# The gate of the second sub-layer applied to the last product instead of to w2 beside the scans

## The chip, the cores and the metric

The kernel runs on one core of a Trainium2 chip, as one program. The metric is the device time of one execution in microseconds (us). Three executions of the kernel before gave 2477.98, 2481.02 and 2481.66 us, so the median is 2481.02 us.

## The reference, cut to what matters

One layer of a hybrid backbone: two token mixers side by side (a bidirectional SSD branch and a bidirectional RG-LRU branch), merged and projected, then a squared-ReLU MLP. Each sub-layer is modulated at its input and gated at its output. All arrays are float32; there are 1024 latent tokens, 1024 model columns and 4096 hidden columns.

```python
def sq_relu_mlp(h, p):
    return jnp.square(jax.nn.relu(h @ p['w_mlp1'] + p['b_mlp1'])) @ p['w_mlp2'] + p['b_mlp2']

mx = [m[:, None, :] for m in modulation(c, w_mod[l], b_mod[l], N_MOD)]
x_mix, _ = token_mixer(modulate(x, mx[0], mx[1]), p, ctx_states, rows, True)
x = layer_norm(DEEPNORM_ALPHA * x + mx[2] * x_mix, ln1_g[l], ln1_b[l])
x = layer_norm(DEEPNORM_ALPHA * x + mx[5] * sq_relu_mlp(modulate(x, mx[3], mx[4]), p), ln2_g[l], ln2_b[l])
```

The change is about `mx[5]`, a row of 1024 numbers, one per model column. It may multiply the columns of `w_mlp2` (called w2 below) ahead of the product, or the columns of the product behind it.

## The kernel before, in words

A matrix product in float32 is made of three TensorE matmuls on split operands (`mm3`, L112): each operand is split into a high part (ScalarE, a copy to fp32r) and a low part (VectorE, a subtraction), and high x high, high x low and low x high are summed in PSUM. TensorE is written PE, VectorE DVE, ScalarE ACT, GpSimd POOL and SyncE SP in the profile's rows. All DMAs of the kernel are issued by SP, in one order.

The work runs in stages, one behind the other, and a scheduler mixes neighbouring stages by priorities. Each engine then executes its own list strictly in the order that the scheduler wrote.

1. The modulation vectors, the first layer norm and the first tiles of the input projection (to about 90 us).
2. The RG-LRU branch (to about 446 us). `mod_chunk` (L386) leaves `mx[5]` in the DRAM row `drow[1]`.
3. The SSD scans (L489 to L595, about 446 to 1363 us): eight groups `g`. A group projects and convolves B, C, two X tiles and z (`proj`, `conv_silu`), and then treats its two X tiles in turn (`tl` 0 and 1). `to_token` (L445) transposes a tile on PE, four 128x128 blocks at a time, into `misc`, the only PSUM buffer of that tag; a DVE copy (L452) moves each batch into `xtm`, and PE can't write the next batch before that. Then come the chunk states `H`, and for each half the decay tiles: SP loads `R` (L549, two buffers, 512 KB), POOL masks it (L554), ACT makes `L` from it (L559), DVE makes `M` (L562, L563), PE multiplies.
4. `gate_w2` (L481) is called at the end of each half of each tile, 32 times: it loads two halves of a 128x1024 tile of w2, multiplies each by the gate row `mxg` on DVE (L486) and stores it to the DRAM tile `dw2[m]`. The halves go through the pool `evp`, which has four 128x512 buffers under the tag `ev`, shared with every other short-lived tile.
5. The SSD product, the LRU product, the merge, the output projection, the second layer norm and the first MLP product (1363 to 2142 us). Its result goes to the DRAM tiles `da`.
6. The second MLP product (2142 to 2475 us) over 32 k tiles. `FRONT` (k tiles 0 to 3) goes first, each of the 16 result tiles as one plain sum over four k tiles (`direct`, L1080); its result is added on DVE to ALPHA times the residual `dx1` (L1097). `PAIRS` (k tiles 4 to 23) goes through `wino`, a seven-product scheme. `TAIL[0]` (24 to 27) and `TAIL[1]` (28 to 31) are plain sums again, added on DVE at L1130 and L1134, and after L1134 comes the last layer norm of that row of tiles. `TAIL[0]` uses the four PSUM buffers `acc`, `TAIL[1]` the three buffers `y`.

`whole` (L1055) and `halves` (L1065) load and split operands for the plain sums, as 128x1024 tiles or as halves. `hook` (L1117) starts the loads of the tails.

Of the kernel before, what the change touches and what calls it, by code (L numbers as in the profile page):

```python
# [9 lines left out]
F32 = mybir.dt.float32  # L10
F32R = mybir.dt.float32r
AF = mybir.ActivationFunctionType
OP = mybir.AluOpType
# [8 lines left out]
ALPHA = 2.0 ** 0.25  # L22
# [33 lines left out]
def _ap(t, off, dims):  # L56
    return bass.AP(tensor=t.tensor, offset=t.offset + off, ap=dims)
# [3 lines left out]
def tile_hybrid_layer(ctx: ExitStack, tc: tile.TileContext, x, xc, wmod, win, wdt, lruw, wbs, wbl,  # L61
# [411 lines left out]
        proj(win[T_Z + t], (0, 1), zcb)  # L473


    dw2 = [dr.tile([128, 1024], F32, name=f"dw{m}") for m in range(32)]
    mxg = [evp.tile([128, 512], F32, tag="ev", name="mxg") for _ in range(2)]
    for h_ in range(2):
        Q.dma_start(mxg[h_], _ap(drow, 1024 + h_ * 512, [[0, 128], [1, 512]]))

    def gate_w2(m):  # L481
        for h_ in range(2):
            sl = slice(h_ * 512, h_ * 512 + 512)
            t_ = evp.tile([128, 512], F32, tag="ev", name="wg")
            Q.dma_start(t_, w2[m][:, sl])
            V.tensor_tensor(t_, t_, mxg[h_], op=OP.mult)  # L486
            Q.dma_start(dw2[m][:, sl], t_)

    z_tile(0)  # L489
    for g in range(8):  # L490
        bf = gp.tile([128, TT], F32, name="bf", bufs=1)
        proj(win[T_B + g], (0, 1, 2), conv_silu(16 + g, bf))
        bt = gp.tile([128, 10, 128], F32, name="bt", bufs=1)
# [15 lines left out]
        for tl in range(2):  # L509
# [29 lines left out]
            for hf_ in range(2):  # L539
# [41 lines left out]
                if tl == 1:  # L581
                    V.tensor_tensor(sq, sq, sqs[0, hf_], op=OP.add)
                    pend.append((g, hf_, sq))
                gate_w2(4 * g + 2 * tl + hf_)
        if g < 7:
            z_tile(2 * g + 2)
            flush()
# [433 lines left out]

    rw0 = ctx.enter_context(tc.tile_pool(name="rw0", bufs=10, reuse_waits="tile"))
    opr = ctx.enter_context(tc.tile_pool(name="opr", bufs=NOP, reuse_waits="tile"))
    ac = ctx.enter_context(tc.tile_pool(name="mlc", bufs=16, side="right", reuse_waits="tile"))
# [9 lines left out]
    def raw1():  # L1036
        return rg.tile([128, 1024], F32, tag="k1", name="k1", bufs=10)
# [11 lines left out]
        return t_  # L1049

    def load_w2(m, t_):
        Q.dma_start(t_, dw2[m])
        return t_

    def whole(m, get):  # L1055

        o_ = []
        for ld in (load_a, load_w2):
            lo, hi = ld(m, get()), get().bitcast(F32R)
            A.activation(hi, lo, AF.Copy)  # L1060
            V.tensor_tensor(lo.bitcast(F32R), lo, hi.bitcast(F32), op=OP.subtract)
            o_.append([(hi[:, h_ * 512:h_ * 512 + 512], lo.bitcast(F32R)[:, h_ * 512:h_ * 512 + 512]) for h_ in range(2)])
        return o_

    def halves(m, pool, tags, bufs):  # L1065
        o_ = []
        for src, (th_, tl_) in zip((da, dw2), tags):
            w_ = []
            for h_ in range(2):
                hi = pool.tile([128, 512], F32R, tag=th_, name=th_, bufs=bufs)  # L1070
                lo = pool.tile([128, 512], F32R, tag=tl_, name=tl_, bufs=bufs)
                raw = lo.bitcast(F32)
                Q.dma_start(raw, src[m][:, h_ * 512:h_ * 512 + 512])
                A.activation(hi, raw, AF.Copy)
                V.tensor_tensor(lo, raw, hi.bitcast(F32), op=OP.subtract)
                w_.append((hi, lo))
            o_.append(w_)
        return o_

    def direct(ops, i, n_, tag="acc", bufs=4):  # L1080
        pt = ps.tile([128, 512], F32, tag=tag, bufs=bufs, name="mo")
        ts_ = slice(i % 4 * 128, i % 4 * 128 + 128)
        for j, (la, rb) in enumerate(ops):
            mm3(pt, la[i // 4][0][:, ts_], la[i // 4][1][:, ts_], rb[n_][0], rb[n_][1], j == 0, j == len(ops) - 1)
        return pt

    with tc.high_priority(offset=60):
        front = [halves(m, mhA, (("mhh", "mhl"), ("mhh", "mhl")), 8) for m in FRONT[:2]]
        front += [whole(m, raw1) for m in FRONT[2:]]
    pre = {}  # L1090
    for r_, c_ in ((0, 0), (1, 0), (0, 1), (1, 1)):
        pre[r_, c_] = [ac.tile([128, 512], F32, name="ma", bufs=16) for i in range(4)]
        for i in range(4):
            t_ = pre[r_, c_][i]
            Q.dma_start(t_, dx1[r_ * 4 + i][:, c_ * 512:c_ * 512 + 512])
            pt = direct(front, r_ * 4 + i, c_)
            V.scalar_tensor_tensor(t_, t_, ALPHA, pt, op0=OP.mult, op1=OP.add)  # L1097

    accs = [pre[{2: (0, 0), 4: (1, 0), 3: (0, 1)}[n]] if n in (2, 4, 3) else
            [mhA.tile([128, 512], F32, tag="mhh" if n in (1, 5) else "mhl", name="ma", bufs=8) for i in range(4)]  # L1100
# [7 lines left out]
        V.tensor_tensor(pre[1, 1][i], pre[1, 1][i], t_, op=OP.add)  # L1108
        return pre[1, 1][i]

    tail = [[], []]

    def tail_raw():
        n0[0] += 1
# [2 lines left out]
    def hook(n):  # L1117
        if n == 7:
            for t_, n_ in ((ln2g, "ln2g"), (ln2b, "ln2b")):
                Q.dma_start(t_, _ap(rows, ROWS[n_] * 1024, [[0, 128], [1, 1024]]))  # L1120
            tail[0] = [whole(m, tail_raw) for m in TAIL[0]]
        else:
            tail[1] = [whole(m, raw1) for m in TAIL[1][:2]]
            tail[1] += [halves(m, opr, (("olh", "oll"), ("orh", "orl")), NOP) for m in TAIL[1][2:]]

    wino(PAIRS, chunks, raw0, raw1_or_w, opr, load_a, load_w2, accs, (2, 3, 4), fin, hook, add5, on=V, bank=1)
    for r_, c_ in ((1, 1), (0, 0), (1, 0), (0, 1)):
        for i in range(r_ * 4, r_ * 4 + 4):
            pt = direct(tail[0], i, c_)
            V.tensor_tensor(macc[i][c_], macc[i][c_], pt, op=OP.add)  # L1130
    for i in (0, 4, 1, 5, 2, 6, 3, 7):
        for n_ in range(2):
            pt = direct(tail[1], i, n_, "y", 3)
# [53 lines left out]
```

## Time and profile before

| what | us |
|---|---|
| median of three runs | 2481.02 |
| the profiled execution | 2482.07 |
| its span | 2480.0 |
| PE busy | 2365.0 |
| DVE busy | 1907.8 |
| ACT busy | 1101.3 |
| POOL busy | 415.7 |

The span is the stretch between the first and the last instruction of the profiled execution; 2.07 us lie around it. A busy engine can still be at less than its full pace: a matmul's row is longer than the time until the next one starts, so a busy time of PE is an upper bound. PEclk is the share of the 2.4 GHz clock that TensorE was granted in a stretch, 1.00 for all of it and 0.5 for a stretch at 1.2 GHz.

### The profile page before, as it was taken

To read this page: it belongs to the slowest core of one execution; us is meant where nothing else is said; L and a number is where in the kernel's file an instruction comes from. 1 tells how busy PE (TensorE), PEld (TensorE's weight loads), DVE (VectorE), ACT (ScalarE), POOL (GpSimd) and SP (SyncE) were. 2 spreads that over 40 slices of the span, in tenths; PEclk is the share of its full clock that TensorE was granted. 3 is DMA by queue.
4 is the path that set the end of the run, shared out by engine and by line. 5 is a ranking of instruction groups with operands and counts; after the bars stand their busy time and mean duration, and the time that the engine had idled before them with its cause. 6 is when DMAs were issued, how large, how long until landed. Compare 5 with 4: busy or idle time off the path is not lost. (4 is left out here: it accounts for less than half of the span.)

```text
span 2480.0 us, 31785 instructions
## 1 busy us (share of the span) xinstructions
PE 2365.0 (95%) x11437; PEld 1888.3 (76%) x11437; DVE 1907.8 (77%) x3206; ACT 1101.3 (44%) x1927; POOL 415.7 (17%) x357
## 2 busy tenths in 40 slices
PE   7999999999999999999999998899979999999998
PEld 3877788777777777777877877677757888788877
DVE  6976788778888888879788489977787555558976
ACT  3666756434343443434344254332245545435521
POOL 1000000001110110101110156600365322000004
PEclk9999999999999999999999999999989999999999
DMA  7322154544544453534333632267224332823121
GB/s 283 127 58 73 56 162 145 174 151 126 176 125 136 130 154 117 167 95 119 93 91 118 230 109 90 77 209 266 85 78 156 119 111 98 295 104 144 43 68 68
DMA packets 149382, 324.11 MB, mean 131 GB/s; under 512 B 16468, under 2 KB 49364, under 8 KB 149224
## 3 DMA queue, kind: packets, MB, share of 16 engines
q1 hardware_dynamic: 149224, 322.08, 40.5%
q8 instruction: 90, 1.47, 0.2%
q14 instruction: 68, 0.56, 0.1%
HBM read 256.41 MB, written 65.61 MB: 130 GB/s over the span
## 5 line engine op out<-in xcount | busy, mean ns | idle before, releaser
L114 PE MATMUL acc<-hl,wh 128*128 128x512 f32 (+1 forms) x1560 | 600.2, 385 | 0.6 <-DVE hl L182 0.6
L113 PE MATMUL acc<-hh,wh 128*128 128x512 f32 (+1 forms) x1560 | 598.2, 384 | 2.4 <-ACT hh L177 2.4
L115 PE MATMUL acc<-hh,wl 128*128 128x512 f32 (+1 forms) x1560 | 597.9, 383 | 0.0
L113 PEld LDWEIGHTS acc<-hh,wh 128*128 128x128 f32 x1560 | 298.4, 191 | 54.2 <-issue 4.1
L114 PEld LDWEIGHTS acc<-hl,wh 128*128 128x128 f32 x1560 | 298.3, 191 | 53.4 <-issue 7.7
L115 PEld LDWEIGHTS acc<-hh,wl 128*128 128x128 f32 x1560 | 298.3, 191 | 53.5 <-issue 8.8
L554 POOL TENSOR_SCALAR_AFFINE_SELECT R<-R 128x512 f32<-128x512 f32 x128 | 90.5, 731 | 1153.0 <-DMA R<-dcum 1118.5
L102 ACT ACTIVATE wh<-wr 128x1024 fp32r<-128x1024 f32 x113 | 119.5, 1057 | 233.4 <-PE acc L114 170.1
L114 PE MATMUL wp<-orl,olh 128*128 128x512 f32 x504 | 200.7, 398 | 23.3 <-DVE orl L622 23.2
L559 ACT ACTIVATE L<-R,cumT 128x128 f32<-128x128 f32 x512 | 162.3, 389 | 124.7 <-issue 63.6
L115 PE MATMUL wp<-orh,oll 128*128 128x512 f32 x504 | 198.9, 395 | 0.0
L113 PE MATMUL wp<-orh,olh 128*128 128x512 f32 x504 | 197.0, 395 | 0.4 <-ACT orh L621 0.2
L103 DVE TENSOR_TENSOR wl<-wr,wh 128x1024 fp32r<-128x1024 f32 x113 | 140.2, 1241 | 23.6 <-ACT wh L102 21.4
L114 PEld LDWEIGHTS wp<-orl,olh 128*128 128x128 f32 x504 | 96.1, 191 | 50.3 <-DVE orl L622 30.2
L537 DVE SCALAR_TENSOR_TENSOR H<-H,dec,misc 128x64 f32<-128x64 f32 x512 | 105.0, 274 | 27.5 <-PE misc L529 23.1
L97 POOL TENSOR_TENSOR mv<-mv,mhalf 128x1 f32<-128x1 f32 x34 | 30.4, 894 | 525.5 <-DVE mv L96 524.4
L621 ACT ACTIVATE olh<-k 128x512 fp32r<-128x512 f32 x108 | 67.9, 628 | 111.7 <-PE wp L114 106.2
L622 DVE TENSOR_TENSOR oll<-k,olh 128x512 fp32r<-128x512 f32 x108 | 89.1, 825 | 32.0 <-ACT olh L621 31.8
L113 PEld LDWEIGHTS wp<-orh,olh 128*128 128x128 f32 x504 | 96.1, 191 | 21.9 <-ACT orh L621 0.6
L115 PEld LDWEIGHTS wp<-orh,oll 128*128 128x128 f32 x504 | 96.2, 191 | 19.6
L622 DVE TENSOR_TENSOR orl<-k,orh 128x512 fp32r<-128x512 f32 x126 | 103.5, 821 | 1.4 <-ACT orh L621 1.4
L899 DVE TENSOR_TENSOR xl<-wr,xh 128x512 fp32r<-128x512 f32 x75 | 74.6, 998 | 32.4 <-ACT xh L898 32.0
(319 smaller groups left out, 4989.0 us busy)
## 6 DMA issues: line engine op xcount, KB each, us to landing
wr<-in_win_dram SPq DMA_DIRECT2D x80, 512.0 KB, 3.6
R<-dcum SPq DMA_DIRECT2D x64, 512.0 KB, 5.6
wr<-in_w_dram SPq DMA_DIRECT2D x37, 512.0 KB, 3.7
wm<-in_wmod_dram SPq DMA_DIRECT2D x32, 512.0 KB, 3.5
wg<-in_w_dram SPq DMA_DIRECT2D x64, 256.0 KB, 3.4
dw<-wg SPq DMA_DIRECT2D x64, 256.0 KB, 3.5
E<-decum SPq DMA_DIRECT2D x64, 256.0 KB, 4.9
da<-r SPq DMA_DIRECT2D x64, 256.0 KB, 2.8
```

Source lines behind the costliest of these rows:

```text
L97: G.tensor_tensor(dst, dst, mhalf[:, :n], op=OP.pow)
L102: A.activation(hi, src, AF.Copy)
L103: V.tensor_tensor(lo, src, hi.bitcast(F32), op=OP.subtract)
L113: P.matmul(pt, wh, mh, start=first, stop=False)
L114: P.matmul(pt, wh, ml, start=False, stop=False)
L115: P.matmul(pt, wl, mh, start=False, stop=last)
L537: V.scalar_tensor_tensor(H[:, k, d_, hs_2], H[:, k - 1, d_, hs_2], dec[:, k, d_ * 32 + 2 * t + h:d_ * 32 + 2 * t + h + 1], sp[:, k - k0, d ...
L554: G.affine_select(out=rv, in_=rv, compare_op=OP.is_ge, fill=-BIG, base=0, pattern=[[0, 2], [0, 2], [sg, 128]], channel_multiplier=-sg)
L559: A.activation(L[:, q], R[:, q, (p % 2) * 128:(p % 2 + 1) * 128], AF.Exp, bias=ncumT[:, p, col:col + 1])
L621: A.activation(hi, src, AF.Copy)
L622: V.tensor_tensor(lo, src, hi.bitcast(F32), op=OP.subtract)
L899: V.tensor_tensor(ts[i][1], v, ts[i][0].bitcast(F32), op=OP.subtract)
```

## The change

`gate_w2` and its 64 loads, 64 multiplications and 64 stores are gone. `wino` reads w2 as it is. The residual is no longer added in the front: the front's result is copied out of PSUM by ACT, and behind the products of `TAIL[0]` each result tile is multiplied by the gate and the residual is added, two more DVE instructions and a load of `dx1` for each of 16 tiles. The last four k tiles come after that, so their w2 is multiplied by the gate on DVE as it is loaded (eight halves, through `evp`). Eight k tiles (0 to 3 and 24 to 27) are copied from w2 to `dw2` in DRAM by eight DMAs that depend on nothing, and are loaded from there.

```diff
-    dw2 = [dr.tile([128, 1024], F32, name=f"dw{m}") for m in range(32)]
-    mxg = [evp.tile([128, 512], F32, tag="ev", name="mxg") for _ in range(2)]
-    for h_ in range(2):
-        Q.dma_start(mxg[h_], _ap(drow, 1024 + h_ * 512, [[0, 128], [1, 512]]))
-
-    def gate_w2(m):
-        for h_ in range(2):
-            sl = slice(h_ * 512, h_ * 512 + 512)
-            t_ = evp.tile([128, 512], F32, tag="ev", name="wg")
-            Q.dma_start(t_, w2[m][:, sl])
-            V.tensor_tensor(t_, t_, mxg[h_], op=OP.mult)
-            Q.dma_start(dw2[m][:, sl], t_)
-
+    dw2 = {m: dr.tile([128, 1024], F32, name=f"dw{m}") for m in (*range(4), *range(24, 28))}
     z_tile(0)
     for g in range(8):
+        m_ = sorted(dw2)[g]
+        Q.dma_start(dw2[m_], w2[m_])
...
-                gate_w2(4 * g + 2 * tl + hf_)
...
     def load_w2(m, t_):
+        Q.dma_start(t_, w2[m])
+        return t_
+
+    def copied(m, t_):
         Q.dma_start(t_, dw2[m])
         return t_
...
-        for src, (th_, tl_) in zip((da, dw2), tags):
+        for q, src in enumerate((da, w2 if gated else dw2)):
...
+                if src is w2:
+                    raw = evp.tile([128, 512], F32, tag="ev", name="wg")
+                    Q.dma_start(raw, w2[m][:, sl])
+                    V.tensor_tensor(raw, raw, gate[0][:, sl], op=OP.mult)
+                else:
+                    raw = lo.bitcast(F32)
+                    Q.dma_start(raw, src[m][:, sl])
                 A.activation(hi, raw, AF.Copy)
                 V.tensor_tensor(lo, raw, hi.bitcast(F32), op=OP.subtract)
...
             t_ = pre[r_, c_][i]
-            Q.dma_start(t_, dx1[r_ * 4 + i][:, c_ * 512:c_ * 512 + 512])
-            pt = direct(front, r_ * 4 + i, c_)
-            V.scalar_tensor_tensor(t_, t_, ALPHA, pt, op0=OP.mult, op1=OP.add)
+            A.activation(t_, direct(front, r_ * 4 + i, c_), AF.Copy)
...
-            tail[1] = [whole(m, raw1) for m in TAIL[1][:2]]
-            tail[1] += [halves(m, opr, (("olh", "oll"), ("orh", "orl")), NOP) for m in TAIL[1][2:]]
+            gate.append(raw1())
+            Q.dma_start(gate[0], _ap(drow, 1024, [[0, 128], [1, 1024]]))
+            tail[1] = [halves(m, of_k1(), True) for m in TAIL[1][:2]]
+            tail[1] += [halves(m, of_opr, True) for m in TAIL[1][2:]]
...
-            pt = direct(tail[0], i, c_)
-            V.tensor_tensor(macc[i][c_], macc[i][c_], pt, op=OP.add)
+            m_, sl = macc[i][c_], slice(c_ * 512, c_ * 512 + 512)
+            r_x = evp.tile([128, 512], F32, tag="ev", name="r1")
+            Q.dma_start(r_x, dx1[i][:, sl])
+            V.tensor_tensor(m_, m_, direct(tail[0], i, c_), op=OP.add)
+            V.tensor_tensor(m_, m_, gate[0][:, sl], op=OP.mult)
+            V.scalar_tensor_tensor(m_, r_x, ALPHA, m_, op0=OP.mult, op1=OP.add)
```

The change shifts the line numbers: the DVE copy of `to_token` stays L452, `M` is L552 and L553 in the changed kernel, and the sums of the two tails are L1148 (with L1149 for the gate and L1150 for the residual) and L1154.

**The order on DVE ahead of the first `to_token` copy of a group.** Before, in the group that starts at 968 us (L486 is the gate, L234 and L236 the convolution, L452 the copy into `xtm`):

```order
L442 SCALAR_TENSOR_TENSOR xf<-th,xf 128x512
L486 TENSOR_TENSOR wg<-wg,mxg 128x512 x2
L234 SCALAR_TENSOR_TENSOR xf<-acc,cw,xf 128x8x63
L234 SCALAR_TENSOR_TENSOR xf<-acc,cw,xf 128x8x62
L236 SCALAR_TENSOR_TENSOR xf<-acc,cw,xf 128x8x63
L452 COPY xtm<-misc 128x512
```

The same place in the changed kernel:

```order
L442 SCALAR_TENSOR_TENSOR xf<-th,xf 128x512
L234 SCALAR_TENSOR_TENSOR xf<-acc,cw,xf 128x8x63
L234 SCALAR_TENSOR_TENSOR xf<-acc,cw,xf 128x8x62
L236 SCALAR_TENSOR_TENSOR xf<-acc,cw,xf 128x8x63
L452 COPY xtm<-misc 128x512
```

Two gates that stood between the convolutions of two segments are gone. From the first such copy of group 0 to that of group 7, the seven lists of the changed kernel on DVE are instruction for instruction (line numbers and buffer numbers aside) the last two of the seven of the kernel before, which hold no gate.

**The order on SP in the scans, ahead of the transposes of a group's second tile.** Before (L485 loads w2 for the gate, L549 is `R`, L543 the decay `E`, L576 stores `du`):

```order
L487 DMA dw_3434<-wg 128x512 x2
L485 DMA wg<-in_w_dram 128x512 x2
L549 DMA R<-dcum 128x4x256
L543 DMA E<-decum 64x2x512
L576 DMA du_3395<-u 128x512
L543 DMA E<-decum 64x2x512
L549 DMA R<-dcum 128x4x256 x2
```

In the changed kernel:

```order
L539 DMA R<-dcum 128x4x256
L533 DMA E<-decum 64x2x512
L566 DMA du_3397<-u 128x512
L533 DMA E<-decum 64x2x512
L539 DMA R<-dcum 128x4x256 x2
```

The two stores and the two loads of the gate that stood ahead of `R` are gone.

**The order on DVE between the last sums of `wino` and the first sum of `TAIL[0]`.** Before, twelve splits (the `k` rows are 128x1024) and then the sum L1130:

```order
L1061 TENSOR_TENSOR k_20408<-k_20408,k_20410 128x1024
L1061 TENSOR_TENSOR k_20413<-k_20413,k_20415 128x1024
L1061 TENSOR_TENSOR k_20418<-k_20418,k_20420 128x1024
L1061 TENSOR_TENSOR k_20423<-k_20423,k_20425 128x1024
L1075 TENSOR_TENSOR oll<-oll,olh 128x512 x2
L1075 TENSOR_TENSOR orl<-orl,orh 128x512 x2
L1075 TENSOR_TENSOR oll<-oll,olh 128x512 x2
L1075 TENSOR_TENSOR orl<-orl,orh 128x512 x2
L1130 TENSOR_TENSOR ma<-ma,mo 128x512 x5
```

In the changed kernel the end of that list (`k_20116` is the gate row; ahead of these rows stand two splits, four gates and two splits more):

```order
L1075 TENSOR_TENSOR tl<-tl,th 128x512 x3
L1075 TENSOR_TENSOR k_20139<-k_20139,k_20138 128x512
L1075 TENSOR_TENSOR k_20147<-wg,k_20146 128x512
L1075 TENSOR_TENSOR k_20139<-k_20139,k_20138 128x512
L1075 TENSOR_TENSOR k_20147<-wg,k_20146 128x512
L1070 TENSOR_TENSOR wg<-wg,k_20116 128x512 x2
L1075 TENSOR_TENSOR tl<-tl,th 128x512
L1075 TENSOR_TENSOR tl<-wg,th 128x512 x2
L1070 TENSOR_TENSOR wg<-wg,k_20116 128x512 x2
L1148 TENSOR_TENSOR ma<-ma,mo 128x512
L1075 TENSOR_TENSOR tl<-wg,th 128x512 x2
L1149 TENSOR_TENSOR ma<-ma,k_20116 128x512
```

Eight gates and 14 splits of 512 columns now stand ahead of the first sum, and two splits behind it. On PE the list changes too: behind the first four products of `TAIL[0]` before come 15 matmuls of `TAIL[1]`, now 30 (parts of three products of `TAIL[1]`, into the three `y` buffers), and only then the fifth product of `TAIL[0]`.

## Rows read from the trace of the kernel before

**Rows 1.** The page's first part: busy us (share of the span) and instructions, each engine.
```profile
PE 2365.0 (95%) x11437; PEld 1888.3 (76%) x11437; DVE 1907.8 (77%) x3206; ACT 1101.3 (44%) x1927; POOL 415.7 (17%) x357
```

**Rows 2.** Busy time by stretch: window, us, busy us per engine (x instructions), PEclk, DMA share, GB/s.
```profile
446.00:517.11 71.11, 66.01 (x325) 55.57 (x324) 49.94 (x74) 23.38 (x44) 4.93 (x8) 0.95 0.65 202
517.11:630.35 113.24, 108.38 (x614) 86.89 (x612) 94.80 (x217) 46.56 (x107) 13.31 (x17) 0.98 0.46 137
630.35:740.34 109.99, 106.25 (x610) 85.39 (x610) 94.62 (x218) 46.04 (x106) 13.10 (x17) 1.00 0.50 144
740.34:852.83 112.49, 108.17 (x610) 86.50 (x610) 95.08 (x217) 46.15 (x106) 13.28 (x17) 0.98 0.48 141
852.83:967.68 114.85, 109.43 (x610) 87.66 (x610) 94.44 (x218) 45.91 (x106) 12.28 (x17) 0.97 0.49 138
967.68:1081.74 114.06, 109.36 (x610) 87.51 (x610) 94.59 (x218) 46.02 (x106) 12.32 (x17) 0.97 0.46 139
1081.74:1190.39 108.65, 107.75 (x607) 86.28 (x608) 89.36 (x207) 46.02 (x106) 13.64 (x17) 0.98 0.33 98
1190.39:1297.77 107.38, 107.13 (x611) 85.51 (x610) 88.82 (x207) 46.21 (x107) 13.59 (x17) 1.00 0.36 99
```

**Rows 3.** Waits of PE, 446 to 1085 us: us in total, times, longest.
```profile
PE misc L450 <- DVE xtm L452: 22.9, 10, 3.4
```

**Rows 4.** Timeline of DVE: start, us, instruction, [idle before it <- what ended it].
```profile
964.13 1.43 DVE L486 TENSOR_TENSOR wg<-wg,mxg 128x512 f32<-128x512 f32 x2 [3.62 <-DMA wg<-in_w_dram]
...
967.68 0.68 DVE L452 COPY xtm<-misc 128x512 f32<-128x512 f32 x1
```

**Rows 5.** Timeline of PE at the same place.
```profile
968.41 1.11 PE L450 MATMUL misc<-ident,xf 128*128 128x128 f32 x4 [2.89 <-DVE xtm L452]
```

**Rows 6.** Timeline of SP: where `R` is issued, with gates and without.
```profile
765.82 0.99 SPq L485 DMA_DIRECT2D wg<-in_w_dram  x2
766.90 0.38 SPq L549 DMA_DIRECT2D R<-dcum  x1
...
1106.87 0.38 SPq L549 DMA_DIRECT2D R<-dcum  x1
```

**Rows 7.** Timeline of POOL: the masks of those two `R`.
```profile
774.62 1.23 POOL L554 TENSOR_SCALAR_AFFINE_SELECT R<-R 128x512 f32<-128x512 f32 x2 [41.43 <-DMA R<-dcum]
...
1112.35 1.54 POOL L554 TENSOR_SCALAR_AFFINE_SELECT R<-R 128x512 f32<-128x512 f32 x2 [37.89 <-DMA R<-dcum]
```

**Rows 8.** Timeline of DVE behind the first of them.
```profile
776.61 0.43 DVE L562 TENSOR_TENSOR M<-L 128x256 f32<-128x256 f32 x1 [3.24 <-ACT L L559]
```

**Rows 9.** Timeline of PE behind the first of them.
```profile
778.44 0.63 PE L450 MATMUL misc<-ident,xf 128*128 128x128 f32 x4 [1.83 <-DVE xtm L452]
```

**Rows 10.** Groups by line, 446 to 1085 us: count | busy us, mean ns | idle before.
```profile
L486 DVE TENSOR_TENSOR wg<-wg,mxg 128x512 f32<-128x512 f32 x64 | 43.2, 686 | 23.0 <-DMA wg<-in_w_dram 20.9 <-DMA dyl<-gq 1.9
```

**Rows 11.** Busy time by stretch, the front of the second MLP product (columns as in 2).
```profile
2147.00:2164.00 17.00, 14.08 (x54) 10.44 (x54) 13.12 (x19) 5.16 (x7) 0.00 (x0) 0.90 1.01 373
```

**Rows 12.** Timeline of PE there.
```profile
2158.47 0.93 PE L113 MATMUL mo<-k,k 128*128 128x512 f32 x2 [2.28 <-ACT k L1060]
```

**Rows 13.** Timeline of PE: the first matmul of `TAIL[0]`.
```profile
2383.94 0.39 PE L113 MATMUL mo<-k,k 128*128 128x512 f32 x1
```

**Rows 14.** Busy time by stretch, `TAIL[0]` (columns as in 2).
```profile
2384.00:2431.00 47.00, 47.00 (x209) 38.93 (x208) 23.91 (x35) 3.25 (x6) 0.00 (x0) 1.00 0.05 17
```

**Rows 15.** Timeline of DVE: the first split of `TAIL[1]` and the first sums of `TAIL[0]`.
```profile
2387.12 4.62 DVE L1061 TENSOR_TENSOR k<-k,k 128x1024 fp32r<-128x1024 f32 x4
...
2396.48 2.48 DVE L1130 TENSOR_TENSOR ma<-ma,mo 128x512 f32<-128x512 f32 x4
```

**Rows 16.** DMA issues by line: count, KB each, median us to landing.
```profile
ma<-dx SPq DMA_DIRECT2D x16, 256.0 KB, 8.1
```

**Rows 17.** Busy time by stretch, early in the kernel (columns as in 2).
```profile
60.00:70.00 10.00, 10.00 (x65) 8.55 (x64) 9.55 (x19) 9.68 (x19) 0.00 (x0) 1.00 0.01 2
```

**Rows 18.** Timeline of ACT: the split of the third projection's weights.
```profile
72.77 1.05 ACT L102 ACTIVATE wh<-wr 128x1024 fp32r<-128x1024 f32 x1
```

More of the change, by code (lines that the diff above doesn't have):

```diff
@@ L1057, in whole @@
         o_ = []
-        for ld in (load_a, load_w2):
+        for ld in (load_a, copied):
             lo, hi = ld(m, get()), get().bitcast(F32R)
@@ L1063, in whole, with halves @@
         return o_
-    def halves(m, pool, tags, bufs):
+    def halves(m, get, gated=False):
         o_ = []
-        for src, (th_, tl_) in zip((da, dw2), tags):
+        for q, src in enumerate((da, w2 if gated else dw2)):
             w_ = []
             for h_ in range(2):
[L1070 to L1073, printed above, removed]
+                hi, lo = get(q)
+                sl = slice(h_ * 512, h_ * 512 + 512)
+                if src is w2:
[5 more added lines that the diff above has]
+                    Q.dma_start(raw, src[m][:, sl])
                 A.activation(hi, raw, AF.Copy)
@@ L1078, in halves, with of_mha, of_opr, of_k1 @@
         return o_
+    def of_mha(q):
+        return [mhA.tile([128, 512], F32R, tag="mh" + c, name="fr" + c, bufs=8) for c in "hl"]
+    def of_opr(q):
+        return [opr.tile([128, 512], F32R, tag="o" + "lr"[q] + c, name="t" + c, bufs=NOP) for c in "hl"]
+    def of_k1():
+        st = []
+        def get(q):
+            if not st:
+                h_, l_ = raw1().bitcast(F32R), raw1().bitcast(F32R)
+                st.extend((h_[:, sl], l_[:, sl]) for sl in (slice(0, 512), slice(512, 1024)))
+            return st.pop(0)
+        return get
     def direct(ops, i, n_, tag="acc", bufs=4):
@@ L1087, in tile_hybrid_layer @@
     with tc.high_priority(offset=60):
-        front = [halves(m, mhA, (("mhh", "mhl"), ("mhh", "mhl")), 8) for m in FRONT[:2]]
+        front = [halves(m, of_mha) for m in FRONT[:2]]
         front += [whole(m, raw1) for m in FRONT[2:]]
@@ L1109, in add5 @@
         return pre[1, 1][i]
-    tail = [[], []]
+    tail, gate = [[], []], []
     def tail_raw():
```

## The prediction, as put on record

> **What bounds the kernel now.** I read the busy times first. TensorE is busy for 95% of the span, VectorE for 77% [rows 1], so the question is what TensorE still waits for where VectorE multiplies w2 by the gate. I cut the scans at the first transpose copy of each group of channels and read busy time by stretch [rows 2]. The seven stretches from group to group do the same work (about 610 matmuls each), but the five with gates in them take 113.24, 109.99, 112.49, 114.85 and 114.06 us, 564.63 in all, and the two behind the last gate 108.65 and 107.38. In the last, TensorE is idle for 0.25 us and its clock is full: that is TensorE's own time for a group. In the five it is idle for 3.7 to 5.4 us, and the granted clock falls to 0.97.
>
> Then the waits of TensorE in that part: one line stands out, ten waits for the copy of the transposes, 22.9 us, the longest 3.4 [rows 3]. Two kinds come in turn, one for each of a group's two tiles.
> - **First tile.** VectorE reaches a pair of gates whose w2 hasn't landed and waits 3.62 us; behind them in its list stand a convolution and the copy, which starts at 967.68 [rows 4]. TensorE, with one buffer for transposes, has waited 2.89 us for it [rows 5].
> - **Second tile.** The load of the decay tile R is issued right behind two loads of w2; the mask that waits for it starts 7.72 us after its issue, against 5.48 us where no gate is left [rows 6, 7]. VectorE then waits 3.24 us for what is made of R [rows 8], the copy stands behind that, and TensorE waits 1.83 us [rows 9].
>
> So the gates cost far more than their 64 times 686 ns [rows 10], and not by VectorE's busy time: by what waits behind them.
>
> **The change, part by part.**
>
> *Scans.* The 64 multiplications and 128 DMAs go. In the changed order VectorE's list from group to group is, seven times over, the list of the two gate-free stretches, and the loads and stores of w2 are gone from ahead of R. I therefore give each of the five stretches 107.38 us: 564.63 - 5 x 107.38 = 27.7 us. The sixth, 108.65, starts inside the last wait; another 1.3 us. Bounds: with 108.65 for each of the five the gain is 21.4 us; it can't be more than 29.0, since at 107.38 TensorE has no gap left.
>
> *Before the first group's copy* (446 to 517 us) TensorE is idle for 5.1 us, and the clock of 0.95 is worth 0.05 x 71.11 = 3.6 us [rows 2]. There is no gate-free twin to compare with, and its order changes more than elsewhere. Ends: 0 and 8.7 us of gain. I take 3, nearer to none, as part of these waits are for convolutions that stay.
>
> *Front of the second product.* Sixteen loads of the residual, 4.19 MB, leave a stretch in which the DMA engines are full (373 GB/s, so 11 us of transfer), TensorE is idle for 2.9 us of 17 and its clock is 0.90, worth 1.7 us [rows 11]; the largest wait is for an operand's split, 2.28 us [rows 12]. Against that, two pair operands (1.05 MB, 2.8 us at that rate) now stand ahead of the last w2 tile. Sixteen sums leave VectorE; sixteen copies go to ACT, which is busy 5.16 us of the 17. Ends: 4.6 us of gain, 3 us of loss. I take a gain of 1.
>
> *Tail.* TensorE starts the first tail at 2383.94 [rows 13]; 209 matmuls in 47 us are 0.225 us each [rows 14]. Four products (48 matmuls) fill the four buffers at 2394.7. VectorE starts the splits at 2387.12 and reaches the first sum at 2396.48 [rows 15]: 9.36 us for what is worth 16 splits of 512 columns, 0.585 us each. Now 8 gates and 14 splits stand ahead of the first sum: 2387.12 + 22 x 0.585 + 0.62 = 2400.6. That would hold TensorE for 5.9 us, but its list now has 30 matmuls of the last tail there, 6.8 us, to 2401.5. So it isn't held, by 0.9 us. After that VectorE has three instructions for each product, 1.9 us against TensorE's 12 x 0.225 = 2.7 us. The residual loads go through four buffers, one round for four products: 8.1 us, their median in the crowded front [rows 16], and 1.9 us of use stay below 10.8 us. In this place the DMA share is 0.05 [rows 14], so they should land sooner. The last four gates reuse buffers that the first four leave at about 8 to 9 us after 2387.12; if their loads took 8.1 us the first sum would be some 5 us late, TensorE would stand for about 4 us, and a slow clock behind it could add 2. Ends: 0 and 6 us of loss; I take 1.
>
> *The eight copies in DRAM* depend on nothing and stand near the start of SP's list, two of them ahead of the weights of the third projection. Nothing in this trace copies from DRAM to DRAM. By the rate of the front, 4.19 MB are 11.2 us if all of it delayed TensorE; but the DMA engines are 1% busy from 60 to 70 us [rows 17], and those weights are first read at 72.77 [rows 18]. Ends: 0 and 11 us; I take 0, from the idle stretch. The loads of w2 from where it lies, in place of dw2, have the same size and places: 0.
>
> *Sum.* -27.7 - 1.3 - 3 - 1 + 1 + 0 = -32.0 us. The profiled execution took 2482.07 us, so 2450.1. It stands 1.05 us above the median of the runs, so I forecast **2449 us**.
>
> **The rivals.**
> - *The second kind of wait stays.* R has two buffers whoever else loads, and VectorE's list still has M ahead of the copy. Then about half of the scans' gain stays away: 27.7 / 2 = 13.9 us, 2463 us. Against it: at 1106.87, with the same two buffers and the same list, the mask came 2.2 us sooner [rows 6, 7] and TensorE shows no such wait. Chance 0.12.
> - *Nothing is won, TensorE being the bound.* Its busy time in a group is 106.3 to 109.4 us with gates and 107.13 without [rows 2]; if the waits only moved to other places of the list, the rest of the sum cancels and the time is 2481 us. Against it stand the two shorter stretches. Chance 0.03. The Trainium skill, Perfetto Trace Analysis, section Identifying the Most-Contended Engine, says to find the engine with the highest occupancy and to improve that one first; taken by the busy column this speaks against relieving VectorE, and would give this rival's 2481 us. The same section warns that busy matmuls say little of how much room there is, and would have the weight loads read in their place; with 76% against 95% [rows 1] the trace agrees with the warning.
> - *Slower: the residual loads pace the tail.* VectorE takes its list in order, so a late residual holds the next sums, the four PSUM buffers fill, and TensorE runs at the pace of the loads. Of four rounds three are exposed; a round takes the load and 1.9 us instead of 10.8. To use up 32 us, and 5 more that a measurement can tell, a load must take 37 / 3 + 10.8 - 1.9 = 21 us; at 22 us the time is 2488 us. Against it: 8.1 us where DMA was full. Chance 0.02.
> - *The front or the start at its bad end*, with the rest as forecast: 2453 to 2460 us. Chance 0.03.
>
> **How the numbers follow.** That leaves 0.80 for the forecast. Its gainful end adds the two bounds above: 29.0 + 8.7 + 4.6 = 42.3 us, less 1.05 for the median, 2439 us (2438.7). The other end reaches to the first rival, 2463 us, which also covers the scans at 21.4 us with a tail of 6 us. A measurement of this kernel tells 0.2%, about 5 us, from no change. Faster by more than that: the forecast, the first rival and the last, 0.95. Within it: 0.03. Slower: 0.02.
>
> **What would show it.** Right: all seven stretches from copy to copy at 107 to 109 us with a granted clock of 0.99 or more; no line in TensorE's waits for the transpose copy above 1 us; the mask of R 5 to 6 us behind its issue; in the tail, the first sum about 13 us behind the first split, and TensorE without a gap there. Wrong: stretches that stay above 110 us (then the waits were not the gates' doing, or came back behind another instruction); a gap of TensorE above 4 us behind the first four tail products; a later first projection at the start; or evictions of the tail more than 2.8 us apart.

## The result, and the profile of the changed kernel

| what | before | changed |
|---|---|---|
| median, us | 2479.50 (4 runs, 2474.97 to 2481.66) | 2440.23 (4 runs, 2438.45 to 2443.13) |
| the profiled execution | 2482.07 | 2443.13 |
| its span | 2480.0 | 2441.3 |

The ratio is 0.9845, with an interval of 0.9827 to 0.9863: the change makes the kernel 39 us faster, where 32 were forecast. In the later series the kernel before stood at 2475.0 to 2475.8 us and the changed kernel's nearest relatives at 2440.8 and 2442.1 (copies_twice and tail_late, below), so the gain is 35 to 39 us.

The page's busy line of the changed kernel, to be held against [rows 1]:

```profile
PE 2353.7 (96%) x11437; PEld 1877.2 (77%) x11437; DVE 1889.2 (77%) x3170; ACT 1112.5 (46%) x1947; POOL 418.3 (17%) x357
```

TensorE issues the same 11437 matmuls and is busy for 11.3 us less, because more of them ran at the full clock (granted over the whole span: 0.987 in place of 0.980). VectorE's share of the span is what it was, 77%. By that line nothing has happened to it.

Busy time by stretch, cut as in [rows 2] at the first transpose copy of each group (same columns: window, us, PE, PEld, DVE, ACT, POOL, PEclk, DMA share, GB/s):

```profile
446.00:507.62 61.62, 60.98 (x318) 51.97 (x317) 40.15 (x57) 23.62 (x44) 4.97 (x8) 1.00 0.33 95
507.62:614.72 107.10, 106.96 (x611) 85.49 (x610) 90.90 (x206) 46.51 (x107) 13.65 (x17) 1.00 0.33 99
614.72:721.99 107.27, 107.03 (x611) 85.42 (x610) 90.24 (x207) 46.39 (x107) 13.69 (x17) 1.00 0.34 99
721.99:829.78 107.79, 107.06 (x611) 85.49 (x610) 89.72 (x206) 46.29 (x107) 13.31 (x17) 1.00 0.37 98
829.78:936.81 107.03, 106.60 (x611) 85.57 (x610) 89.76 (x207) 46.40 (x107) 13.35 (x17) 1.00 0.36 99
936.81:1044.14 107.33, 107.07 (x611) 85.52 (x610) 89.48 (x207) 46.47 (x107) 13.86 (x17) 1.00 0.37 99
1044.14:1151.45 107.31, 106.80 (x611) 85.55 (x610) 89.23 (x206) 46.23 (x107) 13.23 (x17) 1.00 0.36 99
1151.45:1258.85 107.40, 107.06 (x611) 85.48 (x610) 89.06 (x206) 46.40 (x107) 13.35 (x17) 1.00 0.35 99
```

All seven stretches are now what only the last one was: 751.23 us in place of 780.66. The first row is the surprise. From 446 us to the first copy TensorE is idle for 0.64 us, its clock is full, and the copy comes at 507.62 in place of 517.11. Some 1.6 us of that had come about ahead of 446 us, where only the copies in DRAM were added.

Waits of TensorE from 446 to 1259 us, against [rows 3] (us in total, times, longest); the line of the transpose copy has gone from 22.9 us to 0.7:

```profile
PE y L555 <- DVE H L527: 0.8, 2, 0.4
PE misc L450 <- DVE xtm L452: 0.7, 2, 0.6
PE misc L450 <- DVE bf L442: 0.6, 1, 0.6
```

The second product: the first 17 us of the front, the 17 us that begin 5.2 us behind its first matmul as [rows 11] do, and the first 47 us of `TAIL[0]` (against [rows 14]):

```profile
2106.44:2123.44 17.00, 17.00 (x75) 13.76 (x74) 15.46 (x23) 11.30 (x17) 0.00 (x0) 1.00 0.96 364
2111.64:2128.64 17.00, 16.27 (x71) 12.81 (x71) 17.00 (x26) 8.89 (x13) 0.00 (x0) 1.00 0.99 385
2344.71:2391.71 47.00, 47.00 (x209) 38.84 (x208) 44.02 (x72) 7.20 (x12) 0.00 (x0) 1.00 0.40 129
```

The front's DMA engines are about as full as before (0.99 in the place of [rows 11], where they were 1.01), but the residual is no longer among what they carry. TensorE is idle there for 0.73 us, where it was idle for 2.92, and its clock is full. In the tail VectorE has 44.02 us of work in 47 where it had 23.91, and TensorE has no gap.

VectorE's first split and first sum of the tail, against [rows 15]:

```profile
2347.92 1.28 DVE L1075 TENSOR_TENSOR k<-k,k 128x512 fp32r<-128x512 f32 x2
...
2361.16 0.68 DVE L1148 TENSOR_TENSOR ma<-ma,mo 128x512 f32<-128x512 f32 x1
```

The sum starts 13.24 us behind the split (13 were forecast).

### The profile page after: what moved, and what is told of

Its sections match the earlier page's. It is cut to its first block, busy times and chain, and to the rows that moved or that the text cites. A ratio compares the mean times of both kernels' runs of the same rounds, so it can differ in the third digit from the quotient of the medians.

```text
span 2441.3 us, 31541 instructions
## 1 busy us (share of the span) xinstructions
PE 2353.7 (96%) x11437; PEld 1877.2 (77%) x11437; DVE 1889.2 (77%) x3170; ACT 1112.5 (46%) x1947; POOL 418.3 (17%) x357
## 3 DMA queue, kind: packets, MB, share of 16 engines
q8 instruction: 90, 1.47, 0.3%
## 5 line engine op out<-in xcount | busy, mean ns | idle before, releaser
L113 PE MATMUL acc<-hh,wh 128*128 128x512 f32 (+1 forms) x1560 | 591.0, 379 | 2.2 <-ACT hh L177 2.2
L549 ACT ACTIVATE L<-R,cumT 128x128 f32<-128x128 f32 x512 | 163.5, 390 | 126.4 <-issue 58.1
L114 PEld LDWEIGHTS wp<-orl,olh 128*128 128x128 f32 x504 | 95.5, 189 | 52.3 <-DVE orl L611 32.7
L610 ACT ACTIVATE olh<-k 128x512 fp32r<-128x512 f32 x108 | 67.9, 629 | 109.1 <-PE wp L114 107.2
```

The lines of the kernel that those rows point to most:

```text
L113: P.matmul(pt, wh, mh, start=first, stop=False)
L114: P.matmul(pt, wh, ml, start=False, stop=False)
L549: A.activation(L[:, q], R[:, q, (p % 2) * 128:(p % 2 + 1) * 128], AF.Exp, bias=ncumT[:, p, col:col + 1])
L610: A.activation(hi, src, AF.Copy)
```

## The experiments

In each, the stretches are read as above. "Seven stretches" is the sum from the first copy of group 0 to that of group 7.

| kernel | median, us | ratio to before | first copy at | seven stretches |
|---|---|---|---|---|
| before | 2479.5 | 1 | 517.11 | 780.66 |
| changed | 2440.23 | 0.9845 [0.9827, 0.9863] | 507.62 | 751.23 |
| gates_back | 2473.21 | 0.9992 [0.9983, 1.0002] | 515.90 | 773.41 |
| gates_pinned | 2495.70 | 1.0093 [1.0069, 1.0118] | 510.19 | 780.30 |
| mul_alone | 2461.27 | 0.9942 [0.9925, 0.9958] | 508.00 | 755.63 |
| load_alone | 2463.03 | 0.9954 [0.9938, 0.9969] | 508.77 | 757.38 |
| load_store | 2496.08 | 1.0083 [1.0062, 1.0104] | 508.91 | 793.13 |
| thin | 2472.79 | 0.9988 [0.9974, 1.0002] | 509.29 | 766.08 |
| four_bufs | 2455.77 | 0.9925 [0.9909, 0.9941] | 515.47 | 751.93 |
| late_row | 2452.34 | 0.9916 [0.9898, 0.9933] | 509.85 | 761.94 |
| gates_kept | 2449.89 | 0.9901 [0.9885, 0.9918] | 508.14 | 758.60 |
| resid | 2472.03 | 0.9992 [0.9980, 1.0003] | 515.80 | 775.06 |
| copies_twice | 2440.83 | 0.9863 [0.9841, 0.9884] | 509.73 | 749.77 |
| tail_late | 2442.12 | 0.9870 [0.9851, 0.9888] | 509.23 | 750.65 |

**gates_back: one part undone.** `dx2` are scratch tiles in DRAM that nothing reads.

```diff
+    mxg = [evp.tile([128, 512], F32, tag="ev", name="mxg") for _ in range(2)]
...
+            t_ = evp.tile([128, 512], F32, tag="ev", name="wg")
+            Q.dma_start(t_, w2[m][:, sl])
+            V.tensor_tensor(t_, t_, mxg[h_], op=OP.mult)
+            Q.dma_start(dx2[m][:, sl], t_)
...
+                gate_w2(4 * g + 2 * tl + hf_)
```

> The changed kernel with the 64 gates (load, multiplication, store to a scratch tile in DRAM that nothing reads) put back at the end of each half; front, tail and the eight copies stay as changed. Theory (the gates beside the scans are the gain, front and tail are worth about 3 us together): stretches of the five groups with gates at 110 to 115 us again, time 2440 + 29 + 8 = 2477 us, 2472 to 2480. Rival (the stretches became shorter by the other order of the program, not by the gates' absence): stretches of 107 to 108 us, 2440 to 2448 us.

It took 2473.21 us, 33 more than the changed kernel. The head is as long as before (first copy at 515.90), the five stretches with gates take 110.07 to 113.12 us, and only the two behind the last gate take 107.2. Waits of TensorE from 446 to 1290 us:

```profile
PE misc L450 <- DVE xtm L452: 21.0, 10, 3.0
```

So taking the gates out is what won the time; the rival of another order falls.

**What of a gate is it? Four kernels on gates_pinned.** In gates_pinned a copy of one column of `u` ties the load of each gate to its half, so that the planner can't move it and all groups carry eight.

```diff
+            V.tensor_copy(t_[:, 0:1], u[:, 0:1])
             Q.dma_start(t_, w2[m][:, sl])
             V.tensor_tensor(t_, t_, mxg[h_], op=OP.mult)
             Q.dma_start(dx2[m][:, sl], t_)
```

load_store is this without the multiplication, load_alone without multiplication and store, and mul_alone has `V.tensor_tensor(t_, u, mxg[h_], op=OP.mult)` in place of all four lines. In thin that line takes the place of the first, and the other three work on columns 0 to 15 alone.

> The same, but each gate's load is tied to the half that it stands in (a one-column copy of u into the gate's tile comes ahead of the load), so that all eight groups carry eight gates. It is the base for the next two. Theory (DVE waits in its list for a w2 load, and the loads stand ahead of R): all seven stretches at 110 to 114 us, transposes wait for the copy 2 to 3 us twice a group, 2465 to 2480 us. Rival (only the old places were bad): stretches under 108.5 us, 2440 to 2450 us.

> The changed kernel with the 64 multiplications alone, on tiles that are in SBUF already (u times the gate row, result unused), no load and no store of w2. Theory (not VectorE's time but what it waits for): 8 x 0.6 = 4.8 us more of DVE a group hide beside TensorE, stretches 107 to 108.5 us, PE waits for the copy under 1 us each, 2440 to 2448 us. Rival (VectorE's time ahead of the copy is what counts): each stretch 3 to 5 us longer, 110 to 112 us, 2465 to 2480 us.

> The changed kernel with the 64 loads and 64 stores alone (into and out of the same tiles, to a scratch tile in DRAM), no multiplication. Theory with two kinds of wait: the first kind (DVE waits for w2) is gone, the second (R behind the loads of w2 on SP) stays: stretches 108.5 to 110.5 us, the mask of R 7 to 8 us behind its issue, 2450 to 2463 us. Rival A (only VectorE's own wait counts): stretches 107 to 107.8 us, 2440 to 2445 us. Rival B (the traffic is all): stretches 110 to 114 us, 2465 to 2480 us.

> As load_store, without the stores: 64 loads of w2, tied to their halves by a one-column copy, nothing reads them. SP has then no instruction left that waits for a load to land. Theory A (what holds R is SP, which waits with a store until the tile is ready, while R and E stand behind it): stretches 107 to 108.2 us, near mul_alone. Theory B (what holds R is the traffic of the loads themselves on the DMA engines): stretches 109 to 113 us, half or more of what load_store lost.

> The gates tied to their halves with all waits, but load and store only move 16 of 512 columns (8 KB in place of 256 KB); the multiplication of 512 columns is made of u ahead of the load, and the 16 loaded columns are multiplied behind it. Theory A (waiting in order, on SP and on VectorE, for a DMA's latency): most of the loss of gates_pinned stays, stretches 109 to 112 us. Theory B (bytes on the DMA engines): stretches 107.5 to 108.5 us, as mul_alone.

Three of them took longer in all than their theories had it: gates_pinned 2495.70 us (2465 to 2480 expected), mul_alone 2461.27 (2440 to 2448) and load_store 2496.08 (2450 to 2463). Part of that lies behind the seven stretches, where the gates of group 7 stand and the five kernels lose 9 to 20 us more. In mul_alone, from 1300 to 1340 us, TensorE is busy for 28.46 of 40 us (39.69 as far into the last stretch of the changed kernel). The merge's first tile `mg`, which is taken from evp too, is written behind the last gate, 73.6 us into that stretch, in place of 32.7. A shortage of buffers would explain it, but no run separates that. The five are therefore read by their seven stretches. Against the 751.23 us of the changed kernel, 56 gates cost in the seven stretches: all of it 29.1 us, the multiplications alone 4.4, the loads alone 6.1, loads and stores 41.9, the thin gates 14.9. One stretch of mul_alone:

```profile
508.00:616.11 108.11, 106.89 (x611) 85.41 (x610) 94.81 (x214) 46.08 (x107) 15.87 (x17) 1.00 0.33 98
```

VectorE is as busy as with gates (94.81 us) and the stretch is 1 us longer than without. VectorE's time is the smaller part. So are the loads: they cost a seventh of what they cost with stores behind them. But gates_pinned, for all that its seven stretches cost as much as the old gates, loses the time in other places than the kernel before. I had expected TensorE to wait for the transpose copy twice a group; these are its waits from 510 to 1290 us:

```profile
PE misc L450 <- DVE bf L442: 14.0, 7, 3.0
PE y L569 <- DVE H L541: 7.8, 7, 1.6
PE misc L450 <- DVE xtm L452: 2.1, 2, 1.2
```

So the five kernels price gates that stand in these places, and not the ten waits of [rows 3]. In load_store TensorE doesn't wait for the transpose copy either (0.3 us in all). There SP shows what the stores add (its wait for the tiles from 509 to 1302 us; then start, us, instruction):

```profile
SPq L488 <- DMA wg<-in_w_dram: 126.8, 56, 6.7
```

```profile
1212.05 0.95 SPq L487 DMA_DIRECT2D wg<-in_w_dram  x2
1213.06 0.58 SPq L546 DMA_DIRECT2D E<-decum  x1
1217.91 1.69 SPq L488 DMA_DIRECT2D dq<-wg  x2
1219.69 0.99 SPq L552 DMA_DIRECT2D R<-dcum  x2
```

The store can't be issued until the tile has landed, 5.9 us behind the load's issue. SP stands there, and the next `R` behind it, though it needs nothing of the gate. It goes out 34.75 us into the group; in the changed kernel the same `R` goes out at 28.57 of the group that begins at 1151.45:

```profile
1180.02 4.69 SPq L539 DMA_DIRECT2D R<-dcum  x2
```

The thin gates move a thirty-second of the bytes and still cost half, 108.5 to 111.65 us a stretch where theory A had 109 to 112. Their loads of 8 KB took 3.1 us to land (median), those of 256 KB in gates_pinned 5.0. So half of the cost at least isn't bytes; that it is latency waited for in order, on SP and VectorE, is my reading, which no run separates further. My theory of two kinds of wait asked 108.5 to 110.5 us a stretch of load_store; it took up to 117. With the multiplication the planner puts one `R` ahead of the stores, without it none, so that load_store is not simply a part of gates_pinned; the sizes don't add up, and aren't meant to.

**four_bufs: the kernel before with one line changed.** The gate row `mxg` had lived in two of evp's four buffers, which left two for the gates.

```diff
-    mxg = [evp.tile([128, 512], F32, tag="ev", name="mxg") for _ in range(2)]
+    wgp = a2.enter_context(tc.tile_pool(name="wgp", bufs=1, side="right", reuse_waits="tile"))
+    mxg = [wgp.tile([128, 512], F32, tag=f"mx{h_}", name="mxg") for h_ in range(2)]
```

> The kernel before, with the gate row in a pool of its own, so that the gates have all four buffers of evp in place of two. The planned order puts the gates into fewer groups (30, 13, 13 and 8 multiplications in the first four groups, none behind). Theory (a w2 load must come well ahead of its multiplication): VectorE waits less for w2 per gate and the groups behind the fourth are at 107.4 us, so 2455 to 2468 us in all. Rival (the order of loads, stores and R on SP decides, which stays): the four groups with gates grow by as much as the others shrink, 2470 to 2480 us.

2455.77 us, 20 less than before, with every gate still beside the scans. The planner places the gates anew when it has more buffers: 22 stand ahead of the first copy (14 before) and 42 in the first four stretches (50 in the first five before). So what is tested is the buffers together with the order that they allow. Two of the stretches with gates:

```profile
515.47:623.52 108.05, 107.53 (x615) 86.08 (x614) 95.71 (x220) 47.28 (x109) 14.35 (x17) 1.00 0.53 163
623.52:730.23 106.71, 105.83 (x607) 84.93 (x608) 97.07 (x220) 45.21 (x106) 12.64 (x17) 1.00 0.54 163
```

More gates a group than before (97.07 us of VectorE, DMA share 0.54), and 107 us. Waits of VectorE from 516 to 1290 us in gates_back:

```profile
DVE M L565 <- ACT L L562: 16.9, 6, 4.2
DVE wg L487 <- DMA wg<-in_w_dram: 16.8, 10, 3.6
```

The same from 515 to 1268 us in four_bufs, and behind it the transposes' wait there (446 to 1268 us):

```profile
DVE M L563 <- ACT L L560: 9.3, 8, 1.8
DVE wg L487 <- DMA wg<-in_w_dram: 1.8, 2, 1.0
```

```profile
PE misc L450 <- DVE xtm L452: 2.4, 4, 0.8
```

What SP did with two buffers, in gates_back (the group began at 850.42):

```profile
871.30 1.53 SPq L488 DMA_DIRECT2D dq<-wg  x2
874.90 1.00 SPq L486 DMA_DIRECT2D wg<-in_w_dram  x2
876.00 0.38 SPq L552 DMA_DIRECT2D R<-dcum  x1
```

With two buffers a load must wait until the store ahead of it has left the buffer; SP issues nothing from 872.8 to 874.9, `R` behind it goes out 25.6 us into the group (23.6 in the changed kernel), and the load comes so late that VectorE waits for it in its own list. SP's waits of this kind, for a store ahead of a load, in gates_back (446 to 1290 us) and in four_bufs (446 to 1268):

```profile
SPq L486 <- DMA dq<-wg: 76.8, 48, 6.2
SPq L486 <- DMA dw<-wg: 39.7, 37, 3.6
```

The late issue of `R` alone isn't the price: in the four groups with gates in four_bufs the same `R` goes out at 25.1 to 26.3 us, as late as in gates_back (24.9 to 27.7), and TensorE waits at most 0.8 us for a transpose copy. What is gone there is VectorE's wait for w2 and about half of its wait for `L`, and the mask stands 5.2 to 7.0 us behind that `R` in place of 6.6 to 7.9. Which of these counts for how much is not shown. The scans' whole loss, 25 to 29 us, is bought back by two buffers and the order that they allow: 751.93 against 751.23 us. The Trainium skill, Perfetto Trace Analysis, section Optimization Strategy, says that the same gap repeating on the engine that should be saturated can mean that memory for the next tile, a buffer count among other things, is short; here the trace agrees, with ten gaps of up to 3.4 us in [rows 3] that four buffers left at 2.4 us in all.

**late_row and gates_kept: how near do gates beside the scans come?** late_row is four_bufs with the gate row loaded only behind the first half of group 0; gates_kept is that with the residual moved as in resid.

```diff
+                if not (g or tl or hf_):
+                    for h_ in range(2):
+                        V.tensor_copy(mxg[h_][:, 0:1], u[:, 0:1])
+                        Q.dma_start(mxg[h_], _ap(drow, 1024 + h_ * 512, [[0, 128], [1, 512]]))
                 gate_w2(4 * g + 2 * tl + hf_)
```

> four_bufs (gates beside the scans, four buffers for them), and the gate row is loaded only behind the first half of group 0 (a one-column copy of u stands ahead of its load), so that no gate stands ahead of the first group's copy. Theory (the 8 us of the head are the gates and their loads that stand there): the stretch from 446 us to the first copy 62 to 63 us in place of 69.5, the seven stretches behind it 107 to 108.5, 2446 to 2451 us. Rival (the head's stops come from its own convolutions and R, and the clock there is chance): the head stays at 68 us or more, 2454 to 2458 us.

> late_row and the residual moved to the tail as in resid. All gates are still multiplied into w2 beside the scans. Theory (the change's gain is what stood behind the gates, not the gates): 2442 to 2448 us, within 8 us of the changed kernel. Rival (VectorE's 64 multiplications and the 64 stores cost by themselves): above 2450 us.

The head and the first stretch of gates_kept:

```profile
446.00:508.14 62.14, 60.98 (x318) 52.00 (x317) 40.19 (x57) 23.62 (x44) 5.17 (x8) 1.00 0.37 106
508.14:622.10 113.96, 109.31 (x614) 86.89 (x612) 96.27 (x221) 47.06 (x108) 13.44 (x17) 0.99 0.51 152
```

The head is as forecast (62.14 us; 63.85 in late_row, where 62 to 63 were expected and four_bufs has 69.47). The first stretch isn't: VectorE waits for w2 twice in it, 4.9 us, at 560 and 618 us; why these two loads are late is open. Both kernels miss their expected time (2452.34 and 2449.89 us, the latter at the rival's edge), and gates_kept mostly by that stretch: its seven are 7.4 us above those of the changed kernel, 6.9 of them in the first. In the other six, with 50 gates, it takes 644.64 us and the changed kernel 644.13 (late_row 647.00). None of these kernels beats the changed one.

**resid: the residual's move alone**, on the kernel before.

```diff
-            Q.dma_start(t_, dx1[r_ * 4 + i][:, c_ * 512:c_ * 512 + 512])
-            pt = direct(front, r_ * 4 + i, c_)
-            V.scalar_tensor_tensor(t_, t_, ALPHA, pt, op0=OP.mult, op1=OP.add)
+            A.activation(t_, direct(front, r_ * 4 + i, c_), AF.Copy)
...
-            V.tensor_tensor(macc[i][c_], macc[i][c_], pt, op=OP.add)
+            V.tensor_tensor(m_, m_, direct(tail[0], i, c_), op=OP.add)
+            V.scalar_tensor_tensor(m_, r_x, ALPHA, m_, op0=OP.mult, op1=OP.add)
```

> The kernel before, with the residual alone moved: the front's sums are copied out by ACT, and behind the products of TAIL[0] the residual is loaded and added; the gates stay beside the scans. Theory by the ledger of the two traces (front 3.9 us won, tail 0.5 us lost): 2471 to 2473 us where before is 2475 to 2478, a ratio of 0.998 to 0.9995. Rival (front and tail are nothing, the clock there is chance): 0.9995 to 1.001. Rival (the residual loads slow the tail): above 1.001.

0.9992 [0.9980, 1.0003]: the times alone don't tell it from nothing. The traces do. From the first matmul of the front to the first of `TAIL[0]` the kernels with the residual in the front take 242.14 (before), 241.60 (four_bufs) and 243.14 us (late_row); those without it 238.57 (resid), 238.45 (gates_kept), 238.24 (gates_back), 238.26 (changed), 238.92 (copies_twice) and 239.03 (tail_late): 3.7 us by the means. From there to the end it is 96.04 us in the five kernels without gates in the tail, wherever the residual is, and 96.55 to 96.65 in those with eight gates there (tail_late aside): 0.55 us.

**copies_twice: the dose of the eight copies doubled; tail_late: eight copies more on VectorE, ahead of the gates of the tail.**

```diff
         Q.dma_start(dw2[m_], w2[m_])
+        Q.dma_start(dx2[m_], w2[m_])
```

```diff
+                    V.tensor_copy(raw, raw)
                     V.tensor_tensor(raw, raw, gate[0][:, sl], op=OP.mult)
```

> The changed kernel with each of the eight copies in DRAM made twice (the second into tiles that nothing reads). Theory (they run while the DMA engines are idle): 2438 to 2444 us, the convolution of the third projection not more than 1 us later. Rival (each delays the weights behind it): 8 x 0.52 MB at the front's 373 GB/s are 11 us, 2448 to 2452 us.

> The changed kernel with eight more copies of 128x512 on VectorE, in place, each ahead of one of the eight gates of the last four k tiles: 4.8 us more ahead of the first sum of TAIL[0]. The list of TensorE there is the same. Theory (the cover of 30 matmuls is used up but for 0.6 to 0.9 us): TensorE stands for 3.5 to 4.5 us behind them, with a slower clock after it, 2444 to 2447 us. Rival (the cover is larger than it was counted): 2438 to 2442 us.

The copies cost nothing that shows: 2440.83 us. They run in a stretch in which the DMA engines had been almost idle, 60 to 80 us, here in copies_twice:

```profile
60.00:80.00 20.00, 20.00 (x116) 17.10 (x115) 19.29 (x43) 15.80 (x30) 0.00 (x0) 1.00 0.75 242
```

Before, the DMA share there is 0.06; in the changed kernel it is 0.21, and the third projection's weights are read at 72.20; in copies_twice at 72.99, before at 72.77 [rows 18].

tail_late is 1.3 us above copies_twice, of the same series, and its tail 2.4 us longer than that of the changed kernel; it misses the 2444 to 2447 us of its theory, and its stop the 3.5 to 4.5 us. TensorE stands once, for 1.47 us, and for an operand of the last tail whose gate came late, not for the first sum:

```profile
2360.03 1.19 PE L113 MATMUL mo<-th 128*128 128x512 f32 x3 [1.47 <-ACT th L1075]
```

So it doesn't show that the cover of the first sum was nearly used up: that stays a count. And my dose was smaller than I wrote: two copies take 0.67 us from start to start of what follows, not 1.2, so eight take 2.7 us and not 4.8.

```profile
2346.04 0.76 DVE L1070 COPY wg<-wg 128x512 f32<-128x512 f32 x2
2346.71 0.68 DVE L1071 TENSOR_TENSOR wg<-wg,k 128x512 f32<-128x512 f32 x1
```

## Why the prediction was right, and which term was off

The time, 2440.23 us, stands 1.2 us inside the fast end of the range (2439 to 2463): the scans, the head and the front all came out near the ends of most gain, two of them well past the values that I took. The path was right; the size was right for the scans and the tail, and too small by 4 us in the head and by 2.7 in the front.

- **Scans: -29.0 forecast, -29.4 in the two traces.** Right, and in the main for the reason given: the busy time of 64 x 686 ns on VectorE was the smaller part (4.4 us for 56 of them in mul_alone), what waited behind the gates was the larger. The bound of 29.0 was a little low, as the seven stretches took 107.32 us on average and not 107.38. The three kernels with the old gates took 780.66, 773.41 and 775.06 us in these stretches and the three without 749.8 to 751.2, so single pairs give 22 to 31, and 25.8 by their means.
- **The second kind of wait was half explained.** I had the mask of `R` late because `R` is issued behind two loads of w2 [rows 6, 7]. That part holds: behind two such loads the mask stands 7.7 us behind `R`'s issue before (median of 5) and 7.0 in load_alone (16), and 5.9 and 5.5 us where none is near. What I left out is that `R` itself goes out late, 24.9 to 28.8 us into the five groups with gates and 23.6 in the changed kernel: SP has stood with the load ahead of it, for a buffer. By load_alone and four_bufs neither delay costs much by itself, though the loads in load_alone stand ahead of other `R`s than that one; how the loss divides is open. Since all of it went, the sum didn't suffer; but I read a cause off two neighbouring rows without asking what the row ahead had waited for, and so missed that one line of the kernel before, two buffers, would have given back the scans without any of the rest. The rival on it (2463 us) is out: in the changed kernel the mask stands 5.5 to 6.5 us behind `R`'s issue and the transposes wait for 0.7 us in all.
- **Head: -3 forecast between 0 and 8.7; it is -7.1.** This is the term that was mis-sized. The first copy came at 515.5 to 517.1 us in the four kernels with gates ahead of it and at 507.6 to 510.2 in the ten without, 516.07 and 508.97 on average. I took 3 "as part of these waits are for convolutions that stay". TensorE's waits there (446 to 517 us) before:

```profile
PE misc L450 <- DVE bf L442: 3.0, 1, 3.0
PE misc L504 <- ACT cb L505: 2.1, 1, 2.1
```

  The convolutions stayed, the first wait shrank to 0.6 us, the second went, and the clock of 0.95 became 1.00. That the gates had made them late is shown by late_row, which moves the gates of four_bufs out of the head: 63.85 us from 446 us to the first copy in place of 69.47. By what chain they did is not read here. A wait on an instruction that stays is no sign that the wait stays.
- **Front: -1 forecast between -4.6 and +3; it is -3.7**, nearer to the good end. The two operands that now stand ahead of the last w2 tile do no harm, with the DMA engines just as full.
- **Tail: +1 forecast, +0.55 measured**, and the first sum 13.24 us behind the first split. The first sum ended at 2361.84; TensorE's 48 and 30 matmuls at 0.227 us, from 2344.71, last to 2362.4, so by this count the cover had 0.6 us left of the 0.9. Residual loads took 3.0 us (median), not the 8.1 of the crowded front; the slower rival is out.
- **Copies: 0 and 0.**
- **The most-contended engine.** The rival that TensorE's busy time leaves nothing to win (2481 us) is out: it is busy for 95% of the span before and 96% after, and the two are 39 us apart. Most of the gain lies in gaps, the rest in TensorE's busy time, which the clock fits (0.97 to 1.00 before, 1.00 after): in the seven stretches TensorE's busy time fell from 756.5 to 748.6 us for the same matmuls.

The terms as measured, 25.8 (scans, means of three kernels each) or 29.4, 7.1, 3.7 and -0.55, make 36.1 to 39.7 us; the two series give 35 and 39. What no term covers lies between the scans and the front, where nothing was changed: 842.1 to 847.6 us in the nine traces without gates in the last two groups, 844.03 before and 847.59 in the changed kernel's.

## What to carry to other kernels

A background job on a busy kernel's engines can cost most by what stands behind its waits, on the engine that computes and on the queue that issues; here its own busy time was the smaller part. Before such a job is moved or taken out, count its buffers: here two more, and the order that they allowed, bought back the scans, and a load that must wait for a store is visible as a gap of the issuing queue ahead of it. And when a job goes, a wait for an instruction that stays may go with it, so price it by its chain and not by its name.

## What the runs showed of the hardware that I had not expected

- Eight copies of 512 KB from DRAM to DRAM took 10.2 us each to land (median), beside 3.6 for a load of the same size, and cost the kernel nothing, even twice over:

```profile
wr<-in_win_dram SPq DMA_DIRECT2D x80, 512.0 KB, 3.6
...
dw<-in_w_dram SPq DMA_DIRECT2D x8, 512.0 KB, 10.2
```

- A copy of 128x512 in SBUF took VectorE 0.335 us from start to start, a multiplication of two tiles of that size 0.60. The Trainium skill, VectorE: DVE Perf Modes, section The perf-mode tier table, has float32 copies in a faster mode than operations on two tensors; the trace agrees, with a ratio of 1.8.
- The granted clock doesn't fall with every stop of TensorE. Before, the two stops in the head came with clocks of 0.79 (470 to 478 us) and 0.90 (500 to 517); in gates_pinned five of the seven stretches keep a clock of 1.00, two of them with stops of 2.79 and 2.98 us, and behind the stop of 1.47 us in tail_late it stayed at 1.00 too. So a stop's length alone did not tell here what it would cost through the clock.
